# First operands of the down projection made inside the last up pair, weight buffers cut to two, and half of a residual spread over the last product

## The chip, the cores and the metric

The kernel runs on one core of one Trainium2 chip. The metric is the device time of one execution in microseconds (us), first instruction to last, with the launch around it. The engines named here are PE (TensorE, matrix products), DVE (VectorE), ACT (ScalarE), POOL (GpSimd) and SP (SyncE, which issues the DMA transfers). Each runs its own list of instructions strictly in order and waits for the others through semaphores, so an instruction that waits holds back everything listed behind it on its engine.

## The reference

One layer of a conditioned hybrid decoder: 1024 tokens, 1024 channels, everything in fp32. A token mixer with an output projection comes first, then a gated MLP. The end of it is what matters here:

```
mix = (g_ssd * y_ssd + g_sc * y_sc) @ w_o           # 1024 x 1024
x = x + gt1 * rmsnorm(mix, mix_post_g)
h = rmsnorm(x, ffn_pre_g) * (1 + sc2) + sh2
u = causal_dwconv(h @ w_up, ffn_conv_w, ffn_conv_b)  # 1024 x 5632
u_gate, u_val = split(u, 2)
f = (silu(u_gate) * u_val) @ w_down                  # 2816 x 1024
x = x + gt2 * rmsnorm(f, ffn_post_g)
```

## The kernel before

**Products.** An fp32 product is three matmuls: each operand is split into a high part, which ACT casts (L130), and a low part, which DVE subtracts (L131); PE then adds high x high, high x low and low x high into one bank. An operand is thus ready only when ACT and then DVE have passed over it. Suffixes h and l (or hi and lo) name the two parts.

**Up projection.** It is done in 22 pairs u0 to u21, each by a seven-product scheme. Weights of a pair are differences t1 to t4 (L193, DVE) and raw quarters 11, 21, 22, split into seven buffers of a pool `ws`; activations lie in `act` and `sx` (f, fs and their halves). `finish` runs the products in the order 1, 5, 2, 6, 7, 3, 4, the fourth in `last4`. The first two pairs start early: their products 5 and 4 (L171 to L173) need only the lower half of the tokens, and PE runs them while the output projection's last rows (`ot`, L941 to L954, four row blocks with square on ACT L376, a small chain on POOL, and two passes on DVE) are still being normalised. Only when these rows are transposed (`f_t`, L391) can ACT make the upper half `f_a` (L394), from which all other up products follow.

After each pair a convolution and a gate (`uv`, L1039 to L1046) make one row block `f_d` in DRAM.

**Down projection.** Seven products d2, d1, d7, d6, d4, d5, d3, each by `down_product`: six steps p0 to p5 over the inner dimension, 24 matmuls in a full step and 12 in p5, into four banks (dx or dy, one for each row block j). The operands f and w of a step are split into the pool `ops`, three buffers for each kind. After the last step `done` reads the four banks. d5 ends in `done22`, which computes rows 4 to 7 of the output: add (L1199), square on ACT (L1177), multiplication by G2 (L1201), a chain of three tiny POOL operations (L1189, L119, L121), scaling with the residual (L1194) and store. d3 ends in `done12`, the same for rows 0 to 3 (L1207). In d3 the last three steps run row block by row block (`held=3`), so that the four banks finish one after the other.

The order on each engine is set by a scheduler that walks the program; a tile that shares bytes with an older one waits for the older one's last reader.

Of the kernel before, what the change touches and what calls it, by code (L numbers as in the profile page):

```python
# [33 lines left out]
def hybrid_kernel(ctx: ExitStack, tc: tile.TileContext, x, pack, row_p, ada_w, w_in,  # L34
# [143 lines left out]
    class Pair:  # L178
# [86 lines left out]
        def finish(self):  # L265
# [766 lines left out]
    for i in range(KF):  # L1032
        us = (early[i] if i < 2 else start(i)).finish()
        vs = []
        for j in range(2):
# [4 lines left out]
            for k in (1, 0):  # L1040
                s = 2 - k
                V.scalar_tensor_tensor(v[:, s:], us[j][:, :T - s], w[:, k:k + 1], v[:, s:], op0=ALU.mult, op1=ALU.add)  # L1042
            if j == 0:
# [273 lines left out]
```

## Time and profile before

| what | value |
|---|---|
| three timed runs | 2042.07, 2046.02, 2046.38 us (median 2046.02) |
| the profiled execution | 2045.67 us, span 2044.0 us, mean granted PE clock 0.994 |
| busy PE / PE weight load / DVE / ACT / POOL | 1993.1 / 1599.2 / 1453.3 / 978.8 / 152.0 us |
| instructions of PE / DVE / ACT | 9476 / 2016 / 1572 |

The span is what lies between the first and the last instruction of the profiled execution; its own time is 1.67 us longer. A timeline row gives the start, the duration, the engine with the line, and in brackets how long the engine had been idle before and what released it. The granted clock (PEclk) is 1.00 at full speed and 0.50 at half speed.

### The profile page before, as it was taken

The numbers are of one execution on the slowest core, as the hardware profiler recorded it, in microseconds if no ns is written. First come the engines' busy times: TensorE is split into PE (matmuls) and PEld (weight loads), VectorE is DVE, ScalarE is ACT, GpSimd is POOL, SyncE is SP. The second block draws the span as 40 slices with busy tenths as digits, with TensorE's granted clock in tenths as the row PEclk, the third lists the DMA queues.
The fourth block names the chain that finished last, engine by engine and source line by source line (L and its number), as shares of the span: only waits on it lengthen the run. The fifth ranks groups of instructions, "written<-read, shape, count | busy, mean of one in ns | idle before, by whom it ended". The sixth has DMA issues, their size and how long they took to land. (4 is left out here: it accounts for less than half of the span.)

```text
span 2044.0 us, 25283 instructions
## 1 busy us (share of the span) xinstructions
PE 1993.1 (98%) x9476; PEld 1599.2 (78%) x9476; DVE 1453.3 (71%) x2016; ACT 978.8 (48%) x1572; POOL 152.0 (7%) x183
## 2 busy tenths in 40 slices
PE   7999999999999999999999999999999999989997
PEld 3788888888887777777887878876888888868886
DVE  4966567767768787786766555378887777767876
ACT  4665455544547656554422442246554454544443
POOL 1200000000002222121000010021000000000002
PEclk9999999999999999999999999999999999999999
DMA  8233223233245556553686567252222222268362
GB/s 298 77 125 120 104 98 120 100 111 120 99 139 208 167 186 206 170 165 127 203 275 230 196 228 266 93 187 71 103 72 93 83 73 93 83 228 282 119 232 98
DMA packets 128426, 308.97 MB, mean 151 GB/s; under 512 B 11184, under 2 KB 40240, under 8 KB 128304
## 3 DMA queue, kind: packets, MB, share of 16 engines
q1 hardware_dynamic: 128304, 307.36, 43.9%
q8 instruction: 74, 1.21, 0.2%
q14 instruction: 48, 0.39, 0.1%
HBM read 241.65 MB, written 65.67 MB: 150 GB/s over the span
## 5 line engine op out<-in xcount | busy, mean ns | idle before, releaser
L1042 DVE SCALAR_TENSOR_TENSOR uv<-u_u,pk,uv 128x1023 f32<-128x1023 f32 (+1 forms) x88 | 107.2, 1279 | 7.4 <-ACT uv L1039 7.4
L130 ACT CAST u_t_hi<-u_t 128x512 fp32r<-128x512 f32 x88 | 54.7, 623 | 119.8 <-PE u_p L172 108.6
L130 ACT CAST wy_hi<-wy_raw 128x1024 fp32r<-128x1024 f32 x32 | 33.6, 1051 | 133.4 <-PE bps L858 83.4
L594 DVE SCALAR_TENSOR_TENSOR xv<-x_u,pk,xv 128x1023 f32<-128x1023 f32 (+2 forms) x72 | 87.1, 1279 | 4.9 <-ACT xv L591 4.9
L725 ACT ACTIVATE E<-E,tokS 128x128 f32<-128x128 f32 x256 | 80.5, 390 | 14.5 <-DMA E<-acs_d 13.8
L130 ACT CAST u_hi<-u_raw 128x512 fp32r<-128x512 f32 x66 | 41.0, 622 | 73.2 <-PE u_p L172 73.2
L131 DVE TENSOR_TENSOR u_t_lo<-u_t,u_t_hi 128x512 fp32r<-128x512 f32 x88 | 60.2, 687 | 21.2 <-ACT u_t_hi L130 21.1
L716 ACT ACTIVATE Cs<-E 128x1024 f32<-128x1024 f32 x28 | 29.7, 1060 | 75.3 <-DMA E<-acs_d 75.2
L131 DVE TENSOR_TENSOR wy_lo<-wy_raw,wy_hi 128x1024 fp32r<-128x1024 f32 x32 | 39.1, 1221 | 37.4 <-ACT wy_hi L130 37.4
L130 ACT CAST x_t_hi<-x_t 128x512 fp32r<-128x512 f32 x48 | 29.9, 624 | 59.2 <-PE x_p L172 33.8
L1039 ACT ACTIVATE uv<-u_u,pk 128x1024 f32<-128x1024 f32 x44 | 52.5, 1238 | 2.3 <-DVE u_u L260 1.7
L737 PE MATMUL y<-E,xdt 128*64 128x128 f32 x512 | 51.1, 279 | 1.6 <-issue 1.6
L1189 POOL TENSOR_TENSOR dss<-dss,dss 128x1 f32<-128x1 f32 x8 | 3.8, 478 | 623.4 <-PE dx L1117 600.0
L130 ACT CAST x_hi<-x_raw 128x512 fp32r<-128x512 f32 x36 | 22.4, 623 | 53.2 <-PE x_p L172 25.2
L131 DVE TENSOR_TENSOR x_t_lo<-x_t,x_t_hi 128x512 fp32r<-128x512 f32 x48 | 32.5, 687 | 21.1 <-ACT x_t_hi L130 21.1
L727 DVE TENSOR_TENSOR E<-E,sm 128x1024 f32<-128x1024 f32 x32 | 41.1, 1286 | 8.5 <-ACT E L726 8.3
L131 DVE TENSOR_TENSOR u_lo<-u_raw,u_hi 128x512 fp32r<-128x512 f32 x66 | 45.0, 684 | 2.6 <-ACT u_hi L130 2.5
L256 DVE TENSOR_TENSOR u_u<-u_p,u_q 128x512 f32<-128x512 f32 x22 | 15.2, 691 | 44.3 <-PE u_p L173 44.3
L723 POOL TENSOR_TENSOR xw<-xdt,tokS 128x512 f32<-128x512 f32 x28 | 32.4, 1157 | 187.6 <-PE st L747 158.8
L765 DVE SCALAR_TENSOR_TENSOR yo<-xb,pk,y 128x128 f32<-128x128 f32 x128 | 39.3, 341 | 7.1 <-PE y L737 6.8
L737 PE MATMUL y<-Cs,state 128*64 128x128 f32 x448 | 43.9, 273 | 0.0
L896 DVE SCALAR_TENSOR_TENSOR gt<-gt,bps 128x512 f32<-128x512 f32 x32 | 20.5, 683 | 32.5 <-PE bps L859 30.2
(1865 smaller groups left out, 6716.2 us busy)
## 6 DMA issues: line engine op xcount, KB each, us to landing
u_raw<-in_w_up_dram SPq DMA_DIRECT2D x44, 512.0 KB, 3.5
E<-acs_d SPq DMA_DIRECT2D x32, 512.0 KB, 4.7
wy_raw<-in_w_ssd_dram SPq DMA_DIRECT2D x32, 512.0 KB, 4.9
x_raw<-in_w_in_dram SPq DMA_DIRECT2D x24, 512.0 KB, 3.4
xbc_d<-xv SPq DMA_DIRECT2D x24, 512.0 KB, 2.8
xb<-xbc_d SPq DMA_DIRECT2D x16, 768.0 KB, 6.3
f_d<-uv SPq DMA_DIRECT2D x22, 512.0 KB, 2.6
dm<-f_d SPq DMA_DIRECT2D x44, 256.0 KB, 6.0
```

The source lines that it names most:

```text
L130: S.copy(hi, src)
L131: V.tensor_sub(lo, src, hi.bitcast(F32))
L594: V.scalar_tensor_tensor(v[:, s:], u[:, :T - s], w[:, k:k + 1], v[:, s:], op0=ALU.mult, op1=ALU.add)
L716: S.activation(Cs, E, AF.Exp)
L723: G.tensor_tensor(xw, xdt, bc(tS[:, 3, hs], 64), op=ALU.mult)
L725: S.activation(E[:, h, :], E[:, h, :], AF.Relu, scale=-1.0, bias=tS[:, 0, g * 8 + h:g * 8 + h + 1])
L727: V.tensor_tensor(E, E, sm.unsqueeze(1).to_broadcast([P, 8, P]), op=ALU.mult)
L737: return PE.matmul(pt[o * 64:o * 64 + 64, j * P:j * P + P], lhs[:, 2 * j + o, :], rhs[:, 2 * j + o, :], start=first, stop=last)
L765: V.scalar_tensor_tensor(yo[:, i, cs], xb[:, i, cs], cv["ssd_d"][:, g * 4 + i:g * 4 + i + 1], pt[:, i * P:(i + 1) * P], op0=ALU.mult, op1= ...
L896: V.scalar_tensor_tensor(gts[o], gts[o], 1.0, ps[:, o, :], op0=ALU.add, op1=ALU.mult)
L1039: S.activation(v, us[j], AF.Identity, scale=w[:, 2:3], bias=cv["ffn_b"][:, t:t + 1])
L1042: V.scalar_tensor_tensor(v[:, s:], us[j][:, :T - s], w[:, k:k + 1], v[:, s:], op0=ALU.mult, op1=ALU.add)
```

## The change

1. For the up pairs of the MLP the pool `sx` is taken in a scope of its own on the right side of the memory, so that it can be closed before the other pools of the phase. The pool `ws` that is opened behind it lies on other bytes than before.
2. In the last pair, the loads of the first two steps of d2 are issued before the pair's products. Before `last4`, `sx` is closed, the pool `ops` is opened on its bytes, and the operands of d2's steps 0 and 1 are made there; `down_product` takes these first.
3. The pool `ops` keeps three buffers for f and has two for w.
4. `done22` keeps the add and the square; the rest of rows 4 to 7 is `finish22`, called in d3 at steps 1 to 4, one row block each.

The bodies of `size`, `two`, `f_load`, `f_raw` and `w_pair` move up unchanged and are left out.

```diff
@@ -262,7 +262,7 @@
                 self.mul(self.bank(1), "22", "t4", False)
                 S.copy(self.out(0, 1), self.bank(1))
 
-        def finish(self):
+        def finish(self, between=None):
             if self.u is None:
                 self.weights("11", "21", "t1", "t2", "22", "t3")
                 if "4" not in self.q:
@@ -270,6 +270,8 @@
             self.weights("t1", "t2", "22", "t3")
             for n in "1526734":
                 if n == "4":
+                    if between is not None:
+                        between()
                     self.last4()
                 elif n != "2" or "2" not in self.done:
                     getattr(self, "p" + n)()
@@ -449,12 +451,17 @@
 
     def pair_scope(banks=True):
         ph = Scope()
-        cur["sx"] = ph.pool("sx", 20)
+        if banks:
+            cur["sx"] = ph.pool("sx", 20)
+        else:
+            sxs.append(Scope())
+            cur["sx"] = sxs[0].pool("sx", 20, side="right")
         cur["ws"] = ph.pool("ws", 7)
         if banks:
             cur["sp"] = ph.psum("b8", 8)
         return ph
 
+    sxs = []
     ph = pair_scope()
 
     tokS = const.tile([P, NCH, 4, 32], F32, name="tokS")
@@ -1029,8 +1036,53 @@
     cur["sp"] = b8
     sums = build_upper(channels(xn, 0, s2, sh2, "f"), A2, keep, "f")
     finish_upper(A2, sums, "f")
+
...
+    def operand(t, tag, p, name):
+        hi = cur["ops"].tile([P, 2, 512], F32R, tag=tag + "h", bufs=3 if tag == "f" else 2, name=name + "h")
+        low = cur["ops"].tile([P, 2, 512], F32R, tag=tag + "l", bufs=3 if tag == "f" else 2, name=name + "l")
+        if isinstance(t, list):
+            for i, u in enumerate(t):
+                split(u, hi[:, i, :], low[:, i, :])
+        else:
+            m = size(p)
+            split(t[:, :m, :], hi[:, :m, :], low[:, :m, :])
+        return hi, low
+
+    made = []
+    dscope = Scope()
+
+    def first_operands():
+        sxs[0].close()
+        cur["ops"] = dscope.pool("ops", 3, side="right", reuse_waits="tile")
+        for p in range(2):
+            made.append((operand(raws2[p][0], "f", p, f"d2f{p}"), operand(raws2[p][1], "w", p, f"d2w{p}")))
+
     for i in range(KF):
-        us = (early[i] if i < 2 else start(i)).finish()
+        p = early[i] if i < 2 else start(i)
+        if i == KF - 1:
+            raws2 = [(f_raw(1, 0, n, "dm12"), w_pair(1, 0, n, "w21")) for n in range(2)]
+        us = p.finish(first_operands if i == KF - 1 else None)
         vs = []
         for j in range(2):
             t = j * KF + i
@@ -1049,47 +1101,13 @@
 
     base.close()
 
-
-    HK = KF // 2
-    NP = (HK + 1) // 2
     ph = Scope()
     sums = ph.pool("sums", NP, reuse_waits="tile")
-    ops_ = ph.pool("ops", 3, reuse_waits="tile")
     qd = ph.pool("qd", 8, reuse_waits="tile")
     gp = ph.pool("gp", 1, reuse_waits="tile")
     X = [bank(f"dx{j}") for j in range(4)]
     Y = [bank(f"dy{j}") for j in range(4)]
     lo, hi_ = slice(0, 512), slice(512, T)
-
...
 
     def plus(p, dst, a, b, op):
         if isinstance(a, list) or isinstance(b, list):
@@ -1120,7 +1138,10 @@
     def down_product(name, ps, first, f_of, w_of, done, held=0, extra=None):
         ops = []
         for p in range(NP):
-            ops.append((operand(f_of(p), "f", p, f"{name}f{p}"), operand(w_of(p), "w", p, f"{name}w{p}")))
+            if made:
+                ops.append(made.pop(0))
+            else:
+                ops.append((operand(f_of(p), "f", p, f"{name}f{p}"), operand(w_of(p), "w", p, f"{name}w{p}")))
             if extra is not None:
                 extra(p)
             if p < NP - held:
@@ -1142,7 +1163,7 @@
             S.copy(store[j], ps[j])
         return done
 
-    q2, q7, ss0, ss2, tt = [], [], [], [], []
+    q2, q7, ss0, ss1, ss2, tt = [], [], [], [], [], []
     a11, s_, t_ = [], [], []
 
     def first11(p):
@@ -1197,9 +1218,13 @@
     def done22(j):
         t = tt[j]
         V.tensor_tensor(t[:, hi_], X[j], q7[j], op=ALU.add)
-        ss = square(t[:, hi_], 4 + j, 1)
-        V.tensor_tensor(t, t, G2, op=ALU.mult)
-        final(4 + j, ss, ss2[j], "a11", [(t, t, slice(0, T))])
+        ss1.append(square(t[:, hi_], 4 + j, 1))
+
+    def finish22(p):
+        for j in {1: (0,), 2: (1,), 3: (2,), 4: (3,)}.get(p, ()):
+            t = tt[j]
+            V.tensor_tensor(t, t, G2, op=ALU.mult)
+            final(4 + j, ss1[j], ss2[j], "a11", [(t, t, slice(0, T))])
 
     def done12(j):
         t = evt(f"dt{j}")
@@ -1224,8 +1249,10 @@
     down_product("d6", X, False, s2, t2, copy_to(X, tt, ""))
     down_product("d4", Y, False, lambda p: f_raw(1, 1, p, "dm22b"), t4, done21, extra=ahead(s1))
     down_product("d5", X, False, s1, t1, done22, extra=ahead(s4))
-    down_product("d3", X, False, s4, lambda p: w_pair(1, 1, p, "w22c"), done12, held=3)
+    down_product("d3", X, False, s4, lambda p: w_pair(1, 1, p, "w22c"), done12, held=3,
+                 extra=finish22)
     ph.close()
+    dscope.close()
     fps.close()
     pss3.close()
```

The DVE list at the end of the output projection, before: `ot0` to `ot3` are the row blocks of the output projection, u0 and u1 the first two pairs. The weights of u0 stand some 30 rows higher up and are not in this piece.

```order
L954 TENSOR_TENSOR ot3_11419<-ops0_3_11124,G1_8626 128x1024
L944 TENSOR_SCALAR ot1_11357<-ot1_11357,o2r1_11400 128x1024
L941 SCALAR_TENSOR_TENSOR ot3_11419<-ot3_11419,or3_11423,xr3_raw_11417 128x1024
L193 TENSOR_TENSOR u1_t1_11584<-u1_1_raw_11582,u1_0_raw_11580 128x512
L193 TENSOR_TENSOR u1_t2_11590<-u1_1_raw_11582,u1_t1_11584 128x512
L944 TENSOR_SCALAR ot2_11388<-ot2_11388,o2r2_11431 128x1024
L193 TENSOR_TENSOR u1_t4_11596<-u1_0_raw_11580,u1_t2_11590 128x512
L131 TENSOR_TENSOR u1_t1_lo_11587<-u1_t1_11584,u1_t1_hi_11586 128x512
L131 TENSOR_TENSOR u1_t2_lo_11593<-u1_t2_11590,u1_t2_hi_11592 128x512
```

And of the changed kernel:

```order
L961 TENSOR_TENSOR ot3_11419<-ops0_3_11124,G1_8626 128x1024
L948 SCALAR_TENSOR_TENSOR ot2_11388<-ot2_11388,or2_11392,xr2_raw_11386 128x1024
L951 TENSOR_SCALAR ot1_11357<-ot1_11357,o2r1_11400 128x1024
L193 TENSOR_TENSOR u0_t1_11514<-u0_1_raw_11281,u0_0_raw_11279 128x512
L948 SCALAR_TENSOR_TENSOR ot3_11419<-ot3_11419,or3_11423,xr3_raw_11417 128x1024
L131 TENSOR_TENSOR u0_t1_lo_11517<-u0_t1_11514,u0_t1_hi_11516 128x512
L193 TENSOR_TENSOR u0_t2_11520<-u0_1_raw_11281,u0_t1_11514 128x512
L951 TENSOR_SCALAR ot2_11388<-ot2_11388,o2r2_11431 128x1024
L193 TENSOR_TENSOR u0_t4_11526<-u0_0_raw_11279,u0_t2_11520 128x512
L131 TENSOR_TENSOR u0_t2_lo_11523<-u0_t2_11520,u0_t2_hi_11522 128x512
L193 TENSOR_TENSOR u0_t3_11544<-u0_1_raw_11281 128x512
L131 TENSOR_TENSOR u0_t4_lo_11529<-u0_t4_11526,u0_t4_hi_11528 128x512
```

All of u0's differences and splits now stand between and behind the passes over `ot`, and u1's stand behind them.

The DVE list from the last pair into d2, before: u21 is the last pair, uv21 its convolution, d2f0 and d2w0 the operands of d2's step 0, dmt an operand that is prepared for d7.

```order
L252 TENSOR_TENSOR u21_u1_14910<-u21_p5_14881,u21_q6_14924 128x512
L1101 TENSOR_TENSOR dmt_0_15015<-w22a_0_15016,w12_0_15018 128x1024
L131 TENSOR_TENSOR d2f0l_15004<-dm12_0_0_14999,d2f0h_15003 128x512
L1042 SCALAR_TENSOR_TENSOR uv21_0_14965<-u21_u0_14909,pk_75,uv21_0_14965 128x1023
L1042 SCALAR_TENSOR_TENSOR uv21_1_14970<-u21_u1_14910,pk_75,uv21_1_14970 128x1023
L1042 SCALAR_TENSOR_TENSOR uv21_0_14965<-u21_u0_14909,pk_75,uv21_0_14965 128x1022
L1042 SCALAR_TENSOR_TENSOR uv21_1_14970<-u21_u1_14910,pk_75,uv21_1_14970 128x1022
L131 TENSOR_TENSOR d2f0l_15004<-dm12_0_1_15001,d2f0h_15003 128x512
L131 TENSOR_TENSOR d2w0l_15012<-w21_0_15009,d2w0h_15011 128x1024
L1046 TENSOR_TENSOR uv21_0_14965<-uv21_0_14965,uv21_1_14970 128x1024
```

And of the changed kernel:

```order
L252 TENSOR_TENSOR u21_u1_14922<-u21_p5_14893,u21_q6_14936 128x512
L131 TENSOR_TENSOR d2f0l_14969<-dm12_0_0_14830,d2f0h_14968 128x512
L131 TENSOR_TENSOR d2f0l_14969<-dm12_0_1_14832,d2f0h_14968 128x512
L131 TENSOR_TENSOR d2w0l_14975<-w21_0_14834,d2w0h_14974 128x1024
L131 TENSOR_TENSOR d2f1l_14979<-dm12_1_0_14836,d2f1h_14978 128x512
L131 TENSOR_TENSOR d2f1l_14979<-dm12_1_1_14838,d2f1h_14978 128x512
L131 TENSOR_TENSOR d2w1l_14985<-w21_1_14840,d2w1h_14984 128x1024
L1119 TENSOR_TENSOR dmt_0_15031<-w22a_0_15032,w12_0_15034 128x1024
L1094 SCALAR_TENSOR_TENSOR uv21_0_15001<-u21_u0_14921,pk_75,uv21_0_15001 128x1023
L1094 SCALAR_TENSOR_TENSOR uv21_1_15006<-u21_u1_14922,pk_75,uv21_1_15006 128x1023
L1094 SCALAR_TENSOR_TENSOR uv21_0_15001<-u21_u0_14921,pk_75,uv21_0_15001 128x1022
L1094 SCALAR_TENSOR_TENSOR uv21_1_15006<-u21_u1_14922,pk_75,uv21_1_15006 128x1022
```

The splits of d2's steps 0 and 1 now come ahead of the convolution of u21, which comes ahead of step 2's splits.

The DVE list at the change from d5 to d3, before: dt4 and dt5 are the first of four row blocks that `done22` adds up.

```order
L131 TENSOR_TENSOR d3w0l_16483<-w22c_0_16480,d3w0h_16482 128x1024
L1199 TENSOR_TENSOR dt4_15952<-dx0_14991,dq7_0_15722 128x512
L131 TENSOR_TENSOR d3f1l_16511<-dms_1_15529,d3f1h_16510 128x1024
L1201 TENSOR_TENSOR dt4_15952<-dt4_15952,G2_15249 128x1024
L1199 TENSOR_TENSOR dt5_15954<-dx1_14992,dq7_1_15724 128x512
L1194 SCALAR_TENSOR_TENSOR dt4_15952<-dt4_15952,dr4_16429,x1r4_16433 128x1024
```

And of the changed kernel:

```order
L1220 TENSOR_TENSOR dt4_15952<-dx0_15023,dq7_0_15722 128x512
L131 TENSOR_TENSOR d3f1l_16471<-dms_1_15529,d3f1h_16470 128x1024
L1220 TENSOR_TENSOR dt5_15954<-dx1_15024,dq7_1_15724 128x512
L1220 TENSOR_TENSOR dt6_15956<-dx2_15025,dq7_2_15726 128x512
L1220 TENSOR_TENSOR dt7_15958<-dx3_15026,dq7_3_15728 128x512
L131 TENSOR_TENSOR d3w0l_16443<-w22c_0_16440,d3w0h_16442 128x1024
```

The low part of d3's first weights, d3w0l, moved from ahead of the four adds to behind them; the multiplications by G2 follow later.

## Rows read from the trace of the kernel before

**Rows 1.** Page, busy time by engine: us, share of the span, instructions

```profile
PE 1993.1 (98%) x9476; PEld 1599.2 (78%) x9476; DVE 1453.3 (71%) x2016; ACT 978.8 (48%) x1572; POOL 152.0 (7%) x183
```

**Rows 2.** Timeline of PE around 1376: start us, us, instruction

```profile
1375.80 0.39 PE L171 MATMUL u_p<-fs_0h,u_t_hi 128*128 128x512 f32 x1
...
1381.24 1.03 PE L391 MATMUL f_t<-ident,ot 128*128 128x128 f32 x8
```

**Rows 3.** Timeline of DVE, same place

```profile
1376.86 1.28 DVE L941 SCALAR_TENSOR_TENSOR ot<-ot,or,xr_raw 128x1024 f32<-128x1024 f32 x1
1378.07 1.22 DVE L954 TENSOR_TENSOR ot<-ops,G 128x1024 f32<-128x1024 f32 x1
1379.20 0.74 DVE L944 TENSOR_SCALAR ot<-ot,o2r 128x1024 f32<-128x1024 f32 x1
```

**Rows 4.** Timeline of ACT, same place

```profile
1390.72 0.62 ACT L130 CAST u_hi<-u_raw 128x512 fp32r<-128x512 f32 x1 [2.83 <-PE u_p L172]
...
1391.72 0.78 ACT L394 ACTIVATE f_a<-f_t,sh_c,sc_c 128x512 f32<-128x512 f32 x1
```

**Rows 5.** Windows: stretch, its us, busy us of PE, PEld, DVE, ACT, POOL, PEclk, DMA

```profile
1396.00:1400.00 4.00, 4.00 (x12) 2.92 (x11) 3.60 (x4) 2.00 (x3) 1.32 (x2) 0.50 0.00 0
```

**Rows 6.** Waits of PE, 1780 to 1860: us in total, times, longest

```profile
PE dy L1116 <- ACT d2w0h L130: 4.9, 1, 4.9
PE dy L1117 <- DVE d2w0l L131: 2.1, 1, 2.1
```

**Rows 7.** Timeline of PE, last pair into d2

```profile
1808.45 0.39 PE L172 MATMUL u_p<-fs_2l,u_hi 128*128 128x512 f32 x1
...
1812.07 0.39 PE L173 MATMUL u_p<-f_7h,u_t_lo 128*128 128x512 f32 x1
1817.38 1.93 PE L1116 MATMUL dy<-d2w0h,d2f0h 128*128 128x512 f32 x4 [4.92 <-ACT d2w0h L130]
...
1827.49 0.39 PE L1116 MATMUL dy<-d2w1h,d2f1h 128*128 128x512 f32 x1
```

**Rows 8.** Timeline of DVE, last pair into d2

```profile
1809.85 0.69 DVE L252 TENSOR_TENSOR u_u<-u_p,u_q 128x512 f32<-128x512 f32 x1 [1.19 <-PE u_p L173]
...
1814.77 4.87 DVE L1042 SCALAR_TENSOR_TENSOR uv<-u_u,pk,uv 128x1023 f32<-128x1023 f32 x4 [0.45 <-ACT uv L1039]
```

**Rows 9.** Timeline of ACT, same place

```profile
1816.28 1.04 ACT L130 CAST d2w0h<-w 128x1024 fp32r<-128x1024 f32 x1
```

**Rows 10.** Windows, same columns, start of d2

```profile
1818.00:1821.00 3.00, 1.31 (x4) 0.50 (x2) 3.00 (x4) 3.00 (x5) 0.00 (x0) 0.50 1.04 379
```

**Rows 11.** Windows, same columns, products d7 and d3

```profile
1881.70:1911.60 29.90, 29.90 (x134) 24.76 (x133) 29.80 (x36) 13.91 (x22) 0.00 (x0) 1.00 0.59 197
...
2001.50:2037.40 35.90, 31.32 (x134) 24.32 (x132) 27.07 (x30) 11.28 (x20) 12.30 (x21) 1.00 0.24 95
```

**Rows 12.** Waits of PE, 1980 to 2044

```profile
PE dx L1116 <- DVE dt L1199: 2.8, 2, 1.5
PE dx L1117 <- DVE d3w1l L131: 1.8, 1, 1.8
```

**Rows 13.** Timeline of PE, start of d3

```profile
2001.57 0.39 PE L1116 MATMUL dx<-d3w0h,d3f0h 128*128 128x512 f32 x1
```

**Rows 14.** Timeline of DVE, adds at the end of d5

```profile
1999.73 0.69 DVE L1199 TENSOR_TENSOR dt<-dx,dq 128x512 f32<-128x512 f32 x1 [2.90 <-PE dx L1118]
2000.34 1.22 DVE L131 TENSOR_TENSOR d3f1l<-dms,d3f1h 128x1024 fp32r<-128x1024 f32 x1
```

**Rows 15.** Timeline of all engines, the tail

```profile
2037.54 0.60 ACT L1177 ACTIVATE scratch<-dx 128x512 bf16<-128x512 f32 x1 [2.71 <-PE dx L1118]
...
2038.26 0.69 DVE L1207 TENSOR_TENSOR dt<-dx,G 128x512 f32<-128x512 f32 x1 [0.81 <-ACT scratch L1177]
...
2038.85 0.55 POOL L121 TENSOR_TENSOR dr<-dr_m,nhalf 128x1 f32<-128x1 f32 x1
...
2040.10 0.75 DVE L1194 SCALAR_TENSOR_TENSOR dt<-dt,dr,x1r 128x512 f32<-128x512 f32 x1
```

More of the change, by code (lines that the diff above doesn't have):

```diff
@@ L1031, in hybrid_kernel, with size, two, f_load @@
     finish_upper(A2, sums, "f")
+    HK = KF // 2
+    NP = (HK + 1) // 2
+    def size(p):
+        return min(2, HK - 2 * p)
+    def two(pool, tag, name):
+        return pool.tile([P, 2, 512], F32, tag=tag, name=name)
+    def f_load(kk, t, p, i, dst):
+        SY.dma_start(dst, f_d[kk * HK + 2 * p + i][:, t * 512:t * 512 + 512])
+        return dst
+    def f_raw(kk, t, p, name):
+        return [f_load(kk, t, p, i, qt(f"{name}_{p}_{i}")) for i in range(size(p))]
+    def w_pair(kk, n, p, name):
+        m, r0 = size(p), (kk * HK + 2 * p) * P
+        raw = rawp.tile([P, T], F32, tag="raw", name=f"{name}_{p}").rearrange("p (m c) -> p m c", m=2)
+        SY.dma_start(raw[:, :m, :], w_down[r0:r0 + m * P, n * 512:n * 512 + 512].rearrange("(m p) c -> p m c", p=P))
+        return raw
+    def operand(t, tag, p, name):
[15 more added lines that the diff above has]
+            made.append((operand(raws2[p][0], "f", p, f"d2f{p}"), operand(raws2[p][1], "w", p, f"d2w{p}")))
     for i in range(KF):
-        us = (early[i] if i < 2 else start(i)).finish()
+        p = early[i] if i < 2 else start(i)
+        if i == KF - 1:
+            raws2 = [(f_raw(1, 0, n, "dm12"), w_pair(1, 0, n, "w21")) for n in range(2)]
+        us = p.finish(first_operands if i == KF - 1 else None)
         vs = []
@@ L1062, in hybrid_kernel @@
     lo, hi_ = slice(0, 512), slice(512, T)
-    def size(p):
-        return min(2, HK - 2 * p)
-    def two(pool, tag, name):
-        return pool.tile([P, 2, 512], F32, tag=tag, name=name)
-    def f_load(kk, t, p, i, dst):
-        SY.dma_start(dst, f_d[kk * HK + 2 * p + i][:, t * 512:t * 512 + 512])
-        return dst
-    def f_raw(kk, t, p, name):
-        return [f_load(kk, t, p, i, qt(f"{name}_{p}_{i}")) for i in range(size(p))]
-    def w_pair(kk, n, p, name):
-        m, r0 = size(p), (kk * HK + 2 * p) * P
-        raw = rawp.tile([P, T], F32, tag="raw", name=f"{name}_{p}").rearrange("p (m c) -> p m c", m=2)
-        SY.dma_start(raw[:, :m, :], w_down[r0:r0 + m * P, n * 512:n * 512 + 512].rearrange("(m p) c -> p m c", p=P))
-        return raw
-    def operand(t, tag, p, name):
-        hi = ops_.tile([P, 2, 512], F32R, tag=tag + "h", name=name + "h")
-        low = ops_.tile([P, 2, 512], F32R, tag=tag + "l", name=name + "l")
-        if isinstance(t, list):
-            for i, u in enumerate(t):
-                split(u, hi[:, i, :], low[:, i, :])
-        else:
-            m = size(p)
-            split(t[:, :m, :], hi[:, :m, :], low[:, :m, :])
-        return hi, low
     def plus(p, dst, a, b, op):
```

## The prediction

> **What bounds the kernel now.** I began with the page's busy times: PE is at work for 98% of the span [rows 1], so the time can change only where PE stands still, or where work is added behind its last matmul. The lists of PE's waits come next, and they lead to three places. At the start of the down projection PE waits 4.9 us for ACT's cast of d2w0h and 2.1 us for DVE's d2w0l [rows 6]. At the change from d5 to d3 it waits for DVE's adds and for d3w1l [rows 12]; the window of d3 is 35.9 us long [rows 11], while its 132 matmuls at 0.227 us are 29.9 us (0.227 is the 5.44 us between the two rows of [rows 2], over 24 matmuls). The third place costs little now: behind the output projection PE goes straight on with u0's 24 matmuls [rows 2], while DVE is still in the passes over `ot` [rows 3]. I then read the timelines of DVE and ACT at these places, since an operand is ready only when both have passed over it.
>
> **The change, part by part.** Start to start, DVE takes 1.21 us for a scalar_tensor_tensor and 1.13 us for a product of 128x1024 elements, at most 0.74 us for a tensor_scalar [rows 3], 0.61 us for a 128x512 operation [rows 14].
>
> *A, the first pairs.* `ws` lies on other bytes, and its first tile there, u0_t1, has to wait until DVE has multiplied ot3, the last row block. So the whole preparation of u0, done early before, moves behind that instruction. From ot3's multiplication, which moves up one place to 1376.86, to the split u1_t4_lo there are 25 DVE instructions: the 12 of the printed piece, ot3's last pass, four more splits of u0, and eight for u1 and u2. They are one product, two scalar_tensor_tensor, three tensor_scalar and 19 of 128x512: 1.1 + 2.4 + 2.2 + 11.6 = 17.3 us, so u1_t4_lo is ready at 1394.2. Ten of the twelve matmuls of u1's product 4 follow (2.3 us), then ACT's cast and copy, 1.0 us from the cast's start to f_a [rows 4]. f_a comes at 1397.5 instead of 1391.72, and everything in the up projection hangs on it. PE has nothing else: u0's 24 matmuls were its cover. I take **+6.0**; between +4 (DVE's chain is shorter by a wait that goes) and +8.5 (ACT's copies of u0's banks come late, and u1's high parts stand behind them on ACT).
>
> *B, the start of d2.* The bytes of `sx` are free after the last matmul that reads fs, at about 1808.9 [rows 7]. ACT, idle there, casts d2f0 (two of about 0.6) and d2w0 (1.04 [rows 9]) by 1811.1. DVE comes from u_u at 1810.5 [rows 8], and splits d2f0 twice (1.2) and d2w0 (1.1) by 1812.8. PE ends the pair at 1812.3 [rows 7] and has four high x high matmuls (0.9 us) in hand. So step 0 runs without a wait, and step 1 starts at 1812.3 + 5.4 = 1817.7 instead of 1827.49 [rows 7]: -9.7. That takes back the half clock as well, which PE had from 1818 to 1821 [rows 10]. Late next is step 2: behind d2w0l DVE has d2f1l, d2w1l, dmt (3.5), the four of uv21 (4.9 [rows 8]), dmt, uv21, d2f2l, d2w2l (4.6): ready at 1825.8. Step 2 could begin at 1823.2, and its four high x high matmuls reach to 1824.1: 1.7 lost. The loads moved ahead of the pair pass through SP before `f_d20`, while it has nothing else to issue; the next weights, w21_2, are loaded behind dmt_0, at about 1816.5, and have 8 us until DVE comes to them. I count no wait for them, and the end of -5 holds one. Sum **-8.0**, between -9.7 and -5.
>
> *C, two buffers for w.* The first weights of a product can be cast only when step 4 of the product before is done with their buffer, that is 12 matmuls or 2.7 us before the new product's start T. Cast and split take 1.04 + 1.2 = 2.3 us, so in three starts (d2 to d1, d7 to d6, d6 to d4) little is lost, 0.7 us together. Where `done` adds on DVE, at d1 to d7, d4 to d5 and d5 to d3, the list puts w0l behind the four adds and f1l. The first add started 1.84 us ahead of T [rows 13, 14]; four adds (2.4), f1l and w0l (1.2 each) end at T + 2.9. Four high x high matmuls cover 0.9: 2.0 us lost each time. For the first two: 4.0, with the 0.7 **+4.7**. If w0l's place in the list were no hindrance it would be +1.5; if the cast also stood behind ACT's squares, +7.
>
> *D, the waits in d3.* Before, 6.0 us are lost there. Now the multiplications by G2 no longer stand between the adds, and the third of the starts above remains, 2.0 us, with 0.1 for step 5, whose weights share their buffer with step 3: **-3.9** (-5 to -2). The 9.6 us of the moved work lie beside 30 us of d3's matmuls; DVE had 27.1 us busy in 35.9 [rows 11].
>
> *E, the tail.* With w5 in the buffer of w3, PE does steps 3 and 4 of all four row blocks first, and step 5 last. The four banks end 9, 7, 5 and 0 matmuls ahead of PE's end instead of 3.4 us apart. Before, the last store's operand was ready 3.4 us behind PE's end: square at 2037.54, multiplication at 2038.26, POOL's chain, the last pass from 2040.10 for 0.75 [rows 15]. Now four such rows queue on DVE: block 0's first scaling can start at about PE's end, then each block takes a multiplication and two scalings, 0.6 + 0.67 + 0.67; the last ends 7.2 us behind PE's end. **+3.8** (+2.5 to +4.5).
>
> Sum: 6.0 - 8.0 + 4.7 - 3.9 + 3.8 = **+2.6**. On the profiled execution of 2045.67 us this gives **2048.3 us**, 2.3 above the median of the runs shown, which is 0.35 above the profiled one. A change of less than 0.2%, 4.1 us, can't be told from none in this kernel.
>
> **A clock that falls in A.** After an idle stretch of 4.9 us and a second of 2.1, PE ran at 0.50, that is 1.2 GHz [rows 7, 10]; it did again from 1396 to 1400 [rows 5]. In A it now stands idle from the eight transposes to u0_t1_hi, about 4 us. The sum has full speed for u0's and u1's 48 matmuls.
> The Trainium skill ("TensorE: Matmul & The Clock Gate", "What's actually happening") says that the throttled clock is the default and only activity releases it; both rows agree. By that rule the idle stretch would leave PE at half speed; this is the third rival.
>
> **The rivals.**
> 1. *A is absorbed: faster.* f_a waited for u1's own product on ACT [rows 4], not for the row blocks, so the list holds it longer than the data do. If DVE and ACT catch up and f_a is not late, the 6.0 go: 2042.3; with C at its lower end as well it is 2039.1, and I take 2041. Against it: f_a still stands behind that copy.
> 2. *Two w buffers throttle d7: slower.* DVE was busy for 29.80 of 29.90 us there [rows 11] and could work ahead; with two buffers each split of w has to wait for a cast that waits for the step two before. If DVE stands still 1.2 us in each of five steps (about the 1.04 of one cast), PE ends 6 us later: 2054.3. It decides when PE waits over 0.5 us for a low part of w in d7's steps 2 to 5. For it: that DVE is full. Against: cast, f's split and w's split are 3.4 us of a step of 5.4.
> 3. *Half clock in A: slower.* 24 of the 48 matmuls on the path at 0.43 instead of 0.227 us: up to +4.9; 0.8 of it lies under DVE's chain: 2052.4.
> 4. *B gives half.* If the casts start only behind the pair's last matmul, at 1812.5, the first operands are ready some 4.5 us later than I have them: 2052.8. Against it: the last reader of fs at 1808.45 [rows 7].
>
> **How the numbers follow.** The forecast has 0.40, rival 1 0.28, rival 2 0.12, rival 3 0.13, rival 4 0.07. The forecast's own range is 2045 to 2051.5. From 2040.5 to 2054 nearly all of it, most of rival 1 and rivals 3 and 4 are inside. Faster by over 0.2% (under 2041.9): most of rival 1 with a little of the forecast, 0.22. Slower (over 2050.1): rivals 2 to 4 but for 0.04, and 0.08 of the forecast, 0.36. The rest, 0.42, is no change.
>
> **What would show it.** A: PE idle for about 4 us ahead of u0's product 5 and f_a about 6 us later behind the last matmul of the output projection than the 15.9 us of before (1375.80 [rows 2] to 1391.72 [rows 4]). B: no wait for d2w0h or d2w0l, one of 1 to 2.5 us for d2w2l. C and D: PE waits of about 2 us for d7w0l, d5w0l and d3w0l. E: 7 instead of 3.4 us from PE's last matmul to DVE's last pass. The forecast is wrong if f_a comes at its old distance, or if PE waits inside the steps of d7.

## The result, and the profile after

The changed kernel takes **2061.16 us** (median of 4 runs, 2060.37 to 2062.06) against 2046.20 (4 runs, 2042.07 to 2048.83) for the kernel before: ratio 1.0075, 95% interval 1.0058 to 1.0093. It is 15 us slower; the forecast was 2048.3, with a range of 2040.5 to 2054. The profiled execution took 2061.34 us, its span is 2059.6.

The table cuts both profiled executions at the same events, read from the timelines of PE, ACT and DVE: each row is the time from one event to the next, start to start. f_a is the first activation that makes the upper half of the tokens; "last two matmuls" is the last row of the output projection in PE's timeline, which holds two.

| stretch | before | after | difference | forecast |
|---|---|---|---|---|
| last two matmuls of the output projection to f_a | 16.38 | 24.53 | +8.15 | +6.0 (A) |
| f_a to the last up matmul | 420.35 | 423.53 | +3.18 | 0 |
| last up matmul to d2, and d2 | 39.90 | 33.31 | -6.59 | -8.0 (B) |
| d1 | 29.92 | 30.19 | +0.27 | +4.7 (C, for d1 to d5 together) |
| d7 | 29.92 | 35.04 | +5.12 | |
| d6 | 29.92 | 30.39 | +0.47 | |
| d4 | 29.92 | 31.77 | +1.85 | |
| d5 | 29.92 | 32.52 | +2.60 | |
| d3 to its last matmul | 35.46 | 32.34 | -3.12 | -3.9 (D) |
| last matmul to DVE's last pass | 3.07 | 6.75 | +3.68 | +3.8 (E) |

The differences add up to 15.6, as do the spans (2059.6 - 2044.0). PE's busy time, first part of the page of after, answers to [rows 1]:

```profile
PE 1997.9 (97%) x9476; PEld 1596.9 (78%) x9476; DVE 1454.6 (71%) x2016; ACT 979.3 (48%) x1572; POOL 155.4 (8%) x183
```

Of the 15.6 us PE is busy for 4.8 more with the same 9476 matmuls, and idle for 10.8 more. So two things went wrong: PE waits longer, and some matmuls take longer.

*The first pairs.* Timelines of after, of PE, DVE and ACT, in this order (start us, us, instruction; in brackets the idle time before it and who ended it); they answer to [rows 2 to 4]:

```profile
1375.39 0.61 PE L928 MATMUL ops<-woh,mix_7l 128*128 128x512 f32 x2
...
1377.54 1.23 DVE L961 TENSOR_TENSOR ot<-ops,G 128x1024 f32<-128x1024 f32 x1 [0.68 <-ACT scratch L378]
...
1384.34 0.75 DVE L951 TENSOR_SCALAR ot<-ot,o2r 128x1024 f32<-128x1024 f32 x1 [0.71 <-POOL o2r L121]
...
1395.72 0.69 DVE L131 TENSOR_TENSOR u_t_lo<-u_t,u_t_hi 128x512 fp32r<-128x512 f32 x1 [0.71 <-ACT u_t_hi L130]
...
1399.92 0.79 ACT L396 ACTIVATE f_a<-f_t,sh_c,sc_c 128x512 f32<-128x512 f32 x1
```

The chain of 25 instructions is there, and three times DVE stands still for 0.7 us: at its start for ACT's square of row block 3, then for POOL's factor of ot2 and for ACT's cast. The split that the forecast had ready at 1394.2 ends at 1396.4, 2.2 later, and f_a comes at 1399.92 instead of 1397.5.

PE runs at half clock here as well. A window of u0's first product, and PE's next wait behind u0 (timeline of PE):

```profile
1382.00:1386.00 4.00, 4.00 (x9) 2.77 (x10) 3.29 (x6) 2.04 (x4) 3.34 (x4) 0.50 0.93 302
```

```profile
1391.93 0.50 PE L171 MATMUL u_p<-fs_0h,u_t_hi 128*128 128x512 f32 x1 [1.29 <-ACT u_t_hi L130]
```

The eight or nine slow matmuls cost f_a nothing, since PE waits for u1's operands behind them anyway.

*The start of d2.* Timeline of PE, after, in answer to [rows 7]:

```profile
1823.45 0.40 PE L173 MATMUL u_p<-f_7h,u_t_lo 128*128 128x512 f32 x1
1823.69 1.08 PE L1134 MATMUL dy<-d2w0h,d2f0h 128*128 128x512 f32 x4
```

Step 0 starts with no wait. PE's waits from 1820 to 1860, in answer to [rows 6] (who waited, for what: us in total, times, longest):

```profile
PE dy L1135 <- DVE d2w2l L131: 1.5, 1, 1.5
PE dy L1134 <- ACT d2w3h L130: 0.7, 1, 0.7
```

The two are 2.2 us where the forecast had 1.7. In d7 the loss is largest. The waits of PE from 1880 to 1900:

```profile
PE dy L1135 <- DVE d7w0l L131: 3.2, 1, 3.2
```

Timelines of DVE and then PE around the start of d7, after:

```profile
1884.60 0.69 DVE L1116 TENSOR_TENSOR dms<-dm,dms 128x512 f32<-128x512 f32 x1 [1.43 <-DMA dm<-f_d]
...
1886.47 0.68 DVE L1202 TENSOR_TENSOR dq<-dx,dq 128x512 f32<-128x512 f32 x1
...
1890.00 1.22 DVE L131 TENSOR_TENSOR d7w0l<-dmt,d7w0h 128x1024 fp32r<-128x1024 f32 x1
...
1886.95 1.07 PE L1134 MATMUL dy<-d7w0h,d7f0h 128*128 128x512 f32 x4
1891.27 0.79 PE L1135 MATMUL dy<-d7w0l,d7f0h 128*128 128x512 f32 x1 [3.25 <-DVE d7w0l L131]
1891.86 0.63 PE L1136 MATMUL dy<-d7w0h,d7f0l 128*128 128x512 f32 x1
...
1894.42 0.48 PE L1136 MATMUL dy<-d7w0h,d7f0l 128*128 128x512 f32 x1
```

The order on DVE is the one that the forecast drew: adds, f1l, adds, then w0l. But the first add starts 0.48 us ahead of d7's first matmul and not 1.84, since DVE has just stood 1.43 us for a load of dm; and so w0l is ready 4.3 us after that matmul instead of 2.9. Then six matmuls take 0.427 us each (1891.86 to 1894.42), behind an idle stretch of 3.2 us: the granted clock is 0.50 there, the lower level of 1.2 GHz. The window of these (us; busy us of PE, PEld, DVE, ACT, POOL; granted clock; DMA share, GB/s):

```profile
1891.90:1894.40 2.50, 2.50 (x7) 1.94 (x6) 2.50 (x4) 0.12 (x2) 0.00 (x0) 0.50 0.79 290
```

PE's waits in the rest, after (in answer to [rows 12]), and the window of d3 (in answer to [rows 11]):

```profile
PE dx L1135 <- DVE d5w0l L131: 2.3, 1, 2.3
PE dy L1135 <- DVE d4w3l L131: 1.5, 1, 1.5
PE dx L1135 <- DVE d3w0l L131: 0.6, 1, 0.6
PE dx L1134 <- DVE dt L1220: 0.3, 1, 0.3
```

```profile
2016.67:2049.01 32.34, 31.25 (x132) 24.20 (x131) 22.41 (x22) 11.54 (x20) 12.01 (x15) 1.00 0.23 90
```

Every wait but one is for a low part of `w`. At the change from d5 to d3 the forecast's picture came as drawn: DVE's first add stands at 2014.83, 1.84 us ahead of d3's first matmul at 2016.67, and PE starts on d3w0l at 2019.64, 2.97 us behind it. The tail, timelines of PE and DVE, in answer to [rows 15]:

```profile
2049.01 0.39 PE L1136 MATMUL dx<-d3w5h,d3f5l 128*128 128x512 f32 x1
...
2055.76 0.75 DVE L1215 SCALAR_TENSOR_TENSOR dt<-dt,dr,x1r 128x512 f32<-128x512 f32 x1
```

Four row blocks queue on DVE, and the last pass starts 6.75 us behind the last matmul.

### The profile page after: what moved, and what is told of

It is laid out like the page before. It is cut to its first block, busy times and chain, and to the rows that moved or that the text cites. A ratio compares the mean times of both kernels' runs of the same rounds, so it can differ in the third digit from the quotient of the medians.

```text
span 2059.6 us, 25276 instructions
## 1 busy us (share of the span) xinstructions
PE 1997.9 (97%) x9476; PEld 1596.9 (78%) x9476; DVE 1454.6 (71%) x2016; ACT 979.3 (48%) x1572; POOL 155.4 (8%) x183
## 5 line engine op out<-in xcount | busy, mean ns | idle before, releaser
L130 ACT CAST x_t_hi<-x_t 128x512 fp32r<-128x512 f32 x48 | 30.0, 624 | 59.1 <-PE x_p L172 33.8
```

Source lines behind the costliest of these rows:

```text
L130: S.copy(hi, src)
```

## The experiments

Three of the four parts can be made alone; the early operands of part 2 need the bytes of part 1. Medians are told with the kernel before measured on the same chip beside them.

**Part 1 alone** (`sx` on the right side, `ws` on other bytes).

```diff
-        cur["sx"] = ph.pool("sx", 20)
...
+            sxs.append(Scope())
+            cur["sx"] = sxs[0].pool("sx", 20, side="right")
...
+    sxs[0].close()
```

> The kernel before with the first part of the change alone: sx on the right side in a scope of its own, so that ws lies on other bytes; nothing else is changed. Theory (bytes): u0's weights wait for the last readers of these bytes, f_a comes 8.2 us later, the first f products lose another 1.1 and the matmuls that read fs from the new place lose 2.1 over the up pairs, as in the changed kernel: +11.4, about 2057.5 us. Rival (forecast): only the early pairs are late, +6, 2052. Second rival: the delay of f_a comes from the early loads of the down projection, not from ws: no change.

Measured: 2057.67 against 2045.47, ratio 1.0056 (1.0044 to 1.0068). The move of bytes alone costs 12 us: f_a comes 24.55 us behind the output projection, as in after, and the up projection takes 423.62. All of A and the loss in the up projection belong to it.

**Part 3 alone** (two buffers for `w`).

```diff
-        hi = ops_.tile([P, 2, 512], F32R, tag=tag + "h", name=name + "h")
+        hi = ops_.tile([P, 2, 512], F32R, tag=tag + "h", bufs=3 if tag == "f" else 2, name=name + "h")
...
```

> The kernel before with two buffers for w in ops instead of three; nothing else is changed. Theory (two buffers): d7 loses some 5 us (d7w0l behind the adds, then half clock), d5 and d3 about 2 each at their starts, and the tail grows by 3.7 because step 5 of d3 comes last for all row blocks: +11, about 2057 us. Rival (loads): d7's long wait comes from the order of the loads that the early operands bring, so the buffers alone cost 2 at d7, 2 at d5, and the tail: +7 to +8, 2053.5. Second rival: DVE and ACT catch up, under +2.

Measured: 2061.51 against 2045.47, ratio 1.0073 (1.0061 to 1.0085): 16 us. Two things are seen. Timeline of PE at the start of d2, of this kernel:

```profile
1809.13 0.39 PE L173 MATMUL u_p<-f_7h,u_t_lo 128*128 128x512 f32 x1
1809.36 0.61 PE L1116 MATMUL dy<-d2w0h,d2f0h 128*128 128x512 f32 x2
```

d2 starts without a wait, although no operand is made early and no pool is moved. With two `w` buffers the operand pool takes 40,960 bytes of a partition, exactly the bytes of `sx`; with three it takes 49,152 and reaches over the first bytes of `ws`, which are read until the last pair's end. The casts of d2f0 begin at 1805.93, 3.2 us ahead of the last up matmul; in the kernel before they begin at 1812.98, 0.9 us behind it. So the 4.9 us that the kernel before loses here come from those 8 KB; that it is the bytes and not the number of buffers is shown by the last kernel below, which has three. And the price of two buffers is paid in d7 and d3. PE's waits in d7, then in d3, and the window of d3:

```profile
PE dy L1117 <- DVE d7w0l L131: 4.6, 1, 4.6
```

```profile
PE dx L1116 <- DVE dt L1199: 6.6, 3, 2.9
PE dx L1117 <- DVE d3w0l L131: 2.9, 1, 2.9
```

```profile
2005.58:2049.16 43.58, 34.06 (x132) 26.07 (x131) 22.89 (x22) 11.64 (x20) 10.15 (x15) 0.84 0.18 67
```

d7 takes 36.47 us here, without the early loads of part 2, and the tail 6.76. So those loads are not what makes d7's load late; what does is not shown.

**Part 4 alone** (`finish22` spread over d3; its code is in the diff of the change).

> The kernel before with the fourth part of the change alone: done22 keeps the add and the square, finish22 is spread over d3; three buffers for w as before. Theory: the 6 us that PE loses in d3 fall to about 1, the tail stays at 3.4 us behind PE's end: -4.5 to -5, about 2041.5 us. Rival: the moved 9.6 us of DVE work delay d3's splits in its later steps, so that PE waits there instead: -2 to 0.

Measured: 2039.14 against 2045.47, ratio 0.9969 (0.9957 to 0.9980): 6.3 us faster. d3 takes 29.77 us from its first to its last matmul instead of 35.46, with no wait of PE in it, and the tail stays at 3.06. The profiled execution took 2045.19, the longest of the seven: the output projection ends 4.9 us later in it than in the kernel before, a part that the edit leaves alone.

**Parts 1 to 3** (the changed kernel without part 4).

```diff
-        ss1.append(square(t[:, hi_], 4 + j, 1))
...
+        ss = square(t[:, hi_], 4 + j, 1)
+        V.tensor_tensor(t, t, G2, op=ALU.mult)
+        final(4 + j, ss, ss2[j], "a11", [(t, t, slice(0, T))])
...
```

> The changed kernel without part 4: the multiplications by G2 stand between the adds at the start of d3 again, as in the kernel before. Theory (part 4 matters more with two w buffers, since a late w0l can't be made up): d3 from its first to its last matmul 43 to 44 us, as in e2_two_w, instead of 32.3: 2072 us. Rival (parts 3 and 4 don't bear on each other; part 4 is worth the 5.7 us that it gave alone): 38 us, 2067.

Measured: 2071.36 against 2044.47, ratio 1.0130 (1.0116 to 1.0143). Window of d3 of this kernel, in answer to the row of after above:

```profile
2012.94:2056.52 43.58, 34.07 (x133) 26.03 (x131) 22.91 (x22) 11.64 (x20) 10.15 (x15) 0.84 0.18 67
```

43.58 us, the same as with part 3 alone. Part 4 takes 11.2 us off d3 where there are two buffers, and 5.7 where there are three. Parts 1 and 3 cost 12.2 and 16.0 alone, 28.2 together; parts 1 to 3 cost 26.9. So the medians leave 1.3 us for the early operands of part 2, which can't be told from nothing, since each of these costs has an interval of some 2.5 us to either side. At d2 they add nothing: d1 begins 33.8 us behind the last up matmul here, and 33.0 with part 3 alone, where two buffers give d2 its early start without them.

**Why A is late.** Two theories for f_a: the wait of `ws`'s first tile until G1's last reader is through, or the order of DVE's list. The edit, against the changed kernel, lets each tile of `ws` wait for its own bytes only:

```diff
-        cur["ws"] = ph.pool("ws", 7)
+        cur["ws"] = ph.pool("ws", 7) if banks else ph.pool("ws", 7, reuse_waits="tile")
```

> The changed kernel, in which the pool ws of the up pairs waits tile by tile for the older tiles under it instead of for all of them. Theory (the wait for the last reader of G1): u0_t1 can be made when the output projection's weights are read, some 4 us earlier, and only the last of ws's buffers waits for ot3: f_a comes 3 to 5 us earlier, 2056 to 2058 us. Rival: DVE's list of 25 instructions sets f_a, not the wait at its start: under 1 us, 2060.5.

Measured: 2061.09, ratio 1.0080 (1.0067 to 1.0093); f_a comes 24.51 us behind the output projection. The theory of the wait falls. Timeline of DVE in this kernel, where ot3 is multiplied and u0 prepared:

```profile
1374.98 1.22 DVE L961 TENSOR_TENSOR ot<-ops,G 128x1024 f32<-128x1024 f32 x1 [0.68 <-ACT scratch L378]
1376.12 1.27 DVE L948 SCALAR_TENSOR_TENSOR ot<-ot,or,xr_raw 128x1024 f32<-128x1024 f32 x1
1377.32 0.74 DVE L951 TENSOR_SCALAR ot<-ot,o2r 128x1024 f32<-128x1024 f32 x1
1377.98 0.68 DVE L193 TENSOR_TENSOR u_t<-u_raw,u_raw 128x512 f32<-128x512 f32 x1
```

The first difference of u0 (u_t) could be made earlier now, and it still stands behind ot3's multiplication and two passes, with no idle time before it: the list has it there. That leaves the order of the list, which the move of `ws` has changed. A kernel with the old order on the new bytes was not tried, so this is argued and not shown.

**The longer matmuls.** The products on `fs` read operands from two pools: those of product 5 and the first two of product 6 lie in `act`, the last two of product 6 and those of 7 and 3 in `sx`. So product 6, 12 matmuls, can be compared with itself. Timelines of PE, before and then after, at its start, its middle and behind its end:

```profile
1609.45 0.39 PE L171 MATMUL u_p<-fs_0h,u_t_hi 128*128 128x512 f32 x1
...
1610.81 0.39 PE L171 MATMUL u_p<-fs_2h,u_t_hi 128*128 128x512 f32 x1
...
1612.17 0.39 PE L171 MATMUL u_p<-fs_0h,u_hi 128*128 128x512 f32 x1
```

```profile
1599.82 0.39 PE L171 MATMUL u_p<-fs_0h,u_t_hi 128*128 128x512 f32 x1
...
1601.18 0.40 PE L171 MATMUL u_p<-fs_2h,u_t_hi 128*128 128x512 f32 x1
...
1602.58 0.39 PE L171 MATMUL u_p<-fs_0h,u_hi 128*128 128x512 f32 x1
...
1608.25 0.39 PE L171 MATMUL u_p<-f_4h,u_t_hi 128*128 128x512 f32 x1
...
1609.64 0.39 PE L171 MATMUL u_p<-f_6h,u_t_hi 128*128 128x512 f32 x1
```

Before, both halves take 1.36 us, 0.227 a matmul. After, the half in `act` takes 1.36 and the half in `sx` 1.40, 0.233 a matmul, at a granted clock of 1.00. Product 5 keeps its 0.227. The matmuls on the moved operands are slow, and so are the first six of the product behind them (1.39 us, 0.232), whose operands were not moved. In the middle of the up projection a pair of 84 matmuls takes 19.34 us instead of 19.21 (medians of 18 pairs), so 22 pairs lose 2.8 of the 3.2 us.

The first guess was alignment: on the right side `sx` starts at a multiple of 32 bytes, not of 64. The edit, with 32 bytes left unused at the right end:

```diff
+            sxs[0].pool("padr", 1, side="right").tile([P, 8], F32, tag="padr", name="padr")
             cur["sx"] = sxs[0].pool("sx", 20, side="right")
```

> The kernel with the first part of the change alone, and 32 bytes per partition left free at the right end of the memory, so that sx starts at an address that is a multiple of 64 as ws and act do; it started at an odd multiple of 32. Theory (alignment): the matmuls that read fs run at 0.227 us again instead of 0.233, the up pairs take 420 to 421.5 us from f_a to their end instead of 423.6; f_a is still 8.2 late: 2 us faster than without the gap, about 2055.5 us. Rival (place): fs is slower in the right half because of what else goes on there, not by the odd 32 bytes: 423.6 again, 2057.7.

Measured: 2055.86 against 2043.95, ratio 1.0059 (1.0046 to 1.0072), up projection 422.77 against 423.62 with part 1 alone and 420.35 before. The guess falls.

**`sx` left in its place, `ws` moved to the right side.** Here parts 2 and 4 are kept. The operands of d2's steps 0 and 1 lie in a small pool on `sx`'s bytes, and the operand pool, with three `w` buffers again, comes to the right side later:

```diff
+            cur["sx"] = sxs[0].pool("sx", 20)
+            cur["ws"] = ph.pool("ws", 7, side="right")
...
+        cur["ops"] = fscope.pool("first", 2, reuse_waits="tile")
...
+    cur["ops"] = dscope.pool("ops", 3, side="right", reuse_waits="tile")
```

> A version meant to keep the gains without the prices: ws on the right, at about its bytes of before, sx on the left as before; the operands of d2's steps 0 and 1 in a pool of two on sx's bytes, and their 48 matmuls issued before the up pools close; then ops with three buffers for f and w on the right; finish22 spread over d3. Theory: f_a and the up pairs as before, d2 starts without a wait (-9.7, half clock gone), no loss at the products' starts, d3 loses 1 instead of 6, tail as before: -14, about 2032 us. Rival (a wait elsewhere): step 2 of d2 waits for buffers on the bytes of the first pool or of ws, or d2's loads come late: -9, 2037.

Measured: 2044.00 against 2045.47, ratio 0.9991 (0.9982 to 1.0000). f_a comes after 16.43 us as in before, d7 to d3 lose little, and the gain is eaten by the up projection: 430.08 us, with every matmul at 0.2333. In d2 one wait is left:

```profile
PE dy L1076 <- ACT d2w2h L130: 1.9, 1, 1.9
```

The second guess was the distance of the two operands' bytes modulo 64. With a pad of 32 bytes on the left too (`act` and `ws` then are a multiple of 64 apart):

```diff
+    padl = ctx.enter_context(tc.tile_pool(name="padl", bufs=1)).tile([P, 8], F32, tag="padl", name="padl")
```

> The version with the first pool on the left, in which the matmuls of the up pairs took 0.2333 us each and the pairs 430 us; here act and sx are moved up by 32 bytes too, so that both operands of these matmuls start at odd multiples of 32. Theory (relative): what costs is that the two operands differ in their address modulo 64; in the down projection both lie at odd multiples of 32 and take 0.2267: pairs 420 to 421 us, about 2034 us in all. Rival (absolute): an odd multiple of 32 costs by itself: 430 us or more, 2044 us.

Measured: 2043.62 against 2043.95, ratio 0.9993 (0.9984 to 1.0001); 0.2325 us for a matmul, up projection 428.69. It falls too.

The same kernel with another split of d2's first operands over the pools, and `ws` 384 bytes from the place of before:

```diff
+            ph.pool("padr", 1, side="right").tile([P, 8], F32, tag="padr", name="padr")
...
+        cur["ops"], cur["bufs"] = fscope.pool("first", 2, reuse_waits="tile"), {"f": 2, "w": 1}
...
+    cur["ops"], cur["bufs"] = dscope.pool("ops", 3, side="right", reuse_waits="tile"), {"f": 3, "w": 3}
+    made[1].append(operand(raws2[1][1], "w", 1, "d2w1"))
```

> A version of the one with the first pool on the left, mended in two places: ws starts at a multiple of 64 (32 bytes free at the right end), and the first pool holds only f and w of d2's step 0 and f of step 1, so that ops doesn't lie on it and step 2's casts don't wait for step 1's matmuls; w of step 1 is made in ops behind the pair. Theory: up pairs 420.3 us, d2 30 us from the pair's end without a wait, the rest as in that version: -14 to -15, about 2031 us. Rival (the next wait): w of step 1 comes behind the pair's last copies and costs PE 1 to 3 us and half clock: 2034 to 2036.

Measured: 2038.96 against 2043.95, ratio 0.9971 (0.9962 to 0.9981). The wait in d2 is gone (d2 takes 31.10 us), the up projection still takes 428.92.

**The distance in larger steps.** In the kernel before, the tiles of `ws` and `act`, of 2048 bytes each, start a multiple of 2048 bytes apart. In the last kernel, with `sx` on the left as before, the distance has a rest of 384. Two pads at the right end put it at 0 and at 128:

```diff
-            ph.pool("padr", 1, side="right").tile([P, 8], F32, tag="padr", name="padr")
+            ph.pool("padr", 1, side="right").tile([P, 104], F32, tag="padr", name="padr")
```

> e8_best with 416 bytes a partition left unused at the right end, so that ws lies on bytes 194112 and up again and its start differs from that of act by a multiple of 2048, as in the kernel before; sx stays at the right side's bytes of e8. Theory (the time of an up matmul hangs on how far the bytes of its two operands are apart, modulo a power of two up to 2048): spacing back at 0.227 us, up projection 420.3 instead of 428.9 us, 2030 us. Rival (it is the allocation side or the order of the instructions, not the bytes): 428 to 429 us stay, 2039 us.

(with 72 in place of 104 for the second)

> e10_rel0 with 288 instead of 416 bytes unused, so that ws and act start 128 bytes apart modulo 2048. If the spacing hangs on the distance modulo 128 or less, the up projection takes 420.3 us as in e10_rel0; if modulo 256 or more, 424 to 429 us. If e10_rel0 has not got 420.3, this run has its value too.

Measured: with a rest of 0, 2030.20 against 2044.47, ratio 0.9924 (0.9910 to 0.9939), and with a rest of 128 one run of 2039.27. Timelines of PE, first of rest 0, then of rest 128:

```profile
1603.24 0.39 PE L171 MATMUL u_p<-fs_0h,u_t_hi 128*128 128x512 f32 x1
...
1605.96 0.39 PE L171 MATMUL u_p<-f_4h,u_hi 128*128 128x512 f32 x1
```

```profile
1606.00 0.39 PE L171 MATMUL u_p<-fs_0h,u_t_hi 128*128 128x512 f32 x1
...
1608.79 0.39 PE L171 MATMUL u_p<-f_4h,u_hi 128*128 128x512 f32 x1
```

These are the 12 matmuls of product 5, on operands in `act`: 2.72 us against 2.79; up projections of 419.91 and 428.49 us. Windows of 330 us in the middle of it, rest 0 and then rest 128, hold 1448 and 1417 matmuls, both at a granted clock of 1.00:

```profile
1450.00:1780.00 330.00, 330.00 (x1448) 270.15 (x1447) 262.29 (x329) 165.23 (x245) 0.00 (x0) 1.00 0.24 83
```

```profile
1450.00:1780.00 330.00, 330.00 (x1417) 265.25 (x1416) 255.88 (x323) 158.90 (x236) 0.00 (x0) 1.00 0.24 83
```

The instructions and their order are the same in both, and in the kernel with a rest of 384; 128 bytes of pad differ between the first two. No place is slow by itself: in the changed kernel the same `ws` is slow with `sx` and not with `act`, and in the down projection of these last kernels both operands lie where the moved `sx` lay, counted modulo 2048, a multiple of 2048 bytes apart, and 132 matmuls take 29.92 us, 0.227 each. So it is the distance of the two operands.

**The short way.** The kernel before with part 4, and the third `w` buffer in a pool of its own, so that the operand pool lies on `sx`'s bytes alone:

```diff
+    ops2 = ph.pool("ops2", 1, reuse_waits="tile")
...
+        pool, n = (ops_, 3) if tag == "f" else (ops2, 1) if p % 3 == 2 else (ops_, 2)
+        hi = pool.tile([P, 2, 512], F32R, tag=tag + "h", bufs=n, name=name + "h")
```

> The kernel before with part 4 (the multiplications by G2 spread over d3) and one change of place: the third w buffer lies in a pool of its own behind the others, so that the pool of the down projection's operands takes 40,960 bytes a partition, exactly those of sx, and no longer reaches over ws. Three w buffers, nothing moved to the right side, no early operands. Theory (d2's first casts waited only because the operand pool lay over ws, whose last reader comes late): step 0 of d2 starts without a wait for d2w0h, 0.2 instead of 5.3 us behind the last up matmul, and d2 itself takes 31 to 33 instead of 34.6; the up projection keeps its 420.3, the tail its 3.1, d3 its 29.8: 2032 to 2034 us. Rival (the early start came from two w buffers, not from the bytes): d2 still starts 5.3 us late, and the time is e3_finish22's, 2039. Second rival: the early casts of d2f0 and d2w0 come in but w2l is late by as much: d2 to d1 34 to 35, 2036.

Measured: **2030.55** against 2044.47, ratio 0.9932 (0.9918 to 0.9945). Timeline of PE, start of d2:

```profile
1808.11 0.39 PE L173 MATMUL u_p<-f_7h,u_t_lo 128*128 128x512 f32 x1
1808.34 0.84 PE L1118 MATMUL dy<-d2w0h,d2f0h 128*128 128x512 f32 x3
```

d2 starts 0.23 us behind the last up matmul, d7 takes 30.54, d3 29.78, the tail 3.06. From the last up matmul to d1 it is 33.66 us instead of 39.90. So d2 gains 6.2 and d3 5.7, together the 11.9 us that the change was forecast to gain there (8.0 and 3.9), without its three costs. Timeline of DVE at the start of d7, whose first matmul is at 1871.69:

```profile
1868.97 1.22 DVE L131 TENSOR_TENSOR d7w0l<-dmt,d7w0h 128x1024 fp32r<-128x1024 f32 x1
...
1873.05 0.68 DVE L1183 TENSOR_TENSOR dq<-dx,dq 128x512 f32<-128x512 f32 x1
```

The first add comes 1.4 us behind that matmul, later than in the changed kernel, and d7 loses only 0.6: with a third buffer d7w0l is split ahead of the adds.

## Why the prediction was wrong

The sum was +2.6, the result +15.6 in the profiled executions. The 13.0 between them are C +5.6, the moved bytes +3.2, A +2.2, B +1.4, D +0.8 and E -0.1. By its steps:

- **C failed most: 4.7 forecast, 10.3 measured** (d1 to d5 in the table). The failed sentence is "The first add started 1.84 us ahead of T", which was read at the change from d5 to d3 and carried over to d7. There the kernel before had its first add 1.22 us ahead, and d7w0l already split. Its timeline of DVE (d7's first matmul is at 1881.89):

```profile
1875.94 1.22 DVE L131 TENSOR_TENSOR d7w0l<-dmt,d7w0h 128x1024 fp32r<-128x1024 f32 x1
...
1880.67 2.48 DVE L1181 TENSOR_TENSOR dq<-dx,dq 128x512 f32<-128x512 f32 x4
```

  After, DVE stood for a load of dm; the add came 1.36 us later than forecast, and so did w0l: a wait of 3.2 us where 2.0 were forecast, and behind it 1.6 us of matmuls at half clock, for which C had no term. Nor did it have one for d4w3l (1.5). The term for d5 was right: 2.0 forecast, 2.3 measured. That part 3 is the cause is shown by the kernel with part 3 alone (d7 36.47 us) and by the last one, with three buffers and the early start (30.54, though its first add is later still).
- **The moved bytes had no term at all: +3.2.** The prediction asked of each edit which wait it makes, and moving a pool makes none in the up projection. There the matmuls on the operands in `sx`, and the few behind them, take 0.232 to 0.234 instead of 0.227 us. Part 1 alone has the same 423.6 us, part 3 alone, with nothing moved, 420.07.
- **A was mis-sized: 6.0 forecast, 8.15 measured,** within its bounds of 4 to 8.5. The 25 instructions were added up as if DVE never waited; it waited three times for 0.7 us. Why the list has this order is not shown.
- **B was mis-sized: -8.0 forecast, -6.6 measured.** The late step 2 is seen (no wait in step 0, no half clock, 1.5 us for d2w2l), with 0.7 for d2w3h beside it. But what the prediction credited to the early operands, the smaller operand pool gives alone, so B credited the wrong part of the change.
- **D and E were right:** -3.1 for -3.9, and +3.7 for +3.8. In d3 the row that was forecast is there: the add 1.84 us ahead, PE on w0l 2.97 us behind the first matmul where 2.9 were forecast.

The rivals: the first (A absorbed) did not come. The second had the right place, d7, and the wrong step: in d7 PE waits for step 0's weights and in none of steps 2 to 5, by which it was to be decided; a wait of that kind came in d4, 1.5 us for d4w3l. The third, half clock in A, came and cost nothing, as PE waited for operands behind it; where half clock did cost, in d7, no rival had it. The fourth did not come. Neither of the two signs by which the prediction wanted to be found wrong came either: f_a was late, and PE did not wait inside d7's later steps.

The range failed because its terms were bounded one by one while they share an engine: what delays DVE in one of them (a load, a cast, POOL's factor) comes on top of every chain that was summed as if it were unbroken.

## What to carry to other kernels

Before operands are made earlier, ask which bytes their pool reaches: here 8 KB too many held back a whole product's start, and taking them away, with part 4, gave the same time as a rearrangement of four places (2030.55 and 2030.20). A chain on a shared engine isn't the sum of its durations when other engines feed it between; add the waits that its kind shows elsewhere in the trace, and the half clock behind any that PE sees. And compare the spacing of matmuls before and after any change of layout: a pool that moves can cost without a single wait.

## What the runs showed of the hardware

The time from one matmul to the next depends here on where the two operands lie in a partition. With weights and moving operand starting a multiple of 2048 bytes apart (each of the four 128-column slices of a weight tile then a multiple of 512) it was 0.227 us; with a rest of 128 or 384 bytes 0.2325, with 416 it was 0.233 to 0.234, all at a granted clock of 1.00. Over an up projection of 420 us this is 8 to 10 us. The distance is not all: in the kernel before, a step of about 0.34 us stands in most pairs where products 3 and 7 are interleaved, and some matmuls behind it are 0.23 to 0.24 us apart at a rest of 0. What inside the chip makes it was not tried, nor other rests, nor matmuls that don't load new weights each time.

The Trainium skill ("TensorE: Matmul & The Clock Gate", "Step-by-step: what each phase is for") says that PE reads the moving operand and the weights through two independent ports, so that loading the next weights takes no bandwidth from the running matmul. By that alone the distance of the two would not matter; the kernels with a rest of 0 and of 128 differ by 128 bytes of pad and by 8.6 us in the up projection, so for this layout the measurement decides, and the page's sentence is not the whole account here.
